# Moving the key eviction to the scalar engine and re-tuning the list scheduler's model in a hybrid attention, convolution and FFN block

## The chip, the cores and the metric

The kernel runs on all eight cores of one Trainium2 chip, two dies of four cores (0 to 3 and 4 to 7). Every core runs the same program on its own share: one of two batches, and eight blocks of 128 query positions. The metric is device microseconds of the slowest core.

Runs come in two states. In the fast one nearly all cores have a mean granted TensorE clock of 0.993 to 0.999 of full speed. In the slow one, one or both dies have a lower clock and the run is longer (31 of the 102 runs whose clocks are on record: 2725 to 3145 us, with the slowest core at a mean clock of 0.814 to 0.979). I compare fast runs only, and in traces I read cores of a die that was not slowed. "Ratio" below means the mean time of one kernel's fast runs over the mean of the kernel before's fast runs of the same rounds, so it is not quite the ratio of the medians that I quote.

Engine names: PE is TensorE (matmuls), PEld its weight loads, ACT the scalar engine, DVE the vector engine, POOL and SP issue DMAs. PSUM is the memory into which PE writes, used by this program as eight banks; "exp" is the exponential of the softmax, done by ACT.

## The reference, cut to what matters

```python
u = rmsnorm(h, ln1_g)
z = u @ w_in                      # conv inputs | q latent | kv latent | k rope | gates
y_conv = (zb * causal_dwconv3(zc * zv, conv_w)) @ w_conv_out
q  = rmsnorm(q_lat) @ w_q_b       # 16 heads x 192
kv = rmsnorm(kv_lat) @ w_kv_b     # per head: 128 key columns (nope), 128 value columns
q, k = rope(rmsnorm(q)), rope(rmsnorm(concat(k_nope, k_rope)))
y_mla = causal_attention(q, k, v) @ w_mla_out      # S = 4096
h = h + (gate_a * y_conv + gate_b * y_mla) @ w_o
h = h + (silu(a_gate) * a_up) @ w_down             # a = dwconv3(rmsnorm(h) @ w_up) + b
```

## The kernel before: the parts that matter here

Three stages follow each other on PE. The *input stage* makes the latents of all 4096 keys. The *attention stage* makes the query latents, then for 16 heads the keys, values, queries, 32 key blocks of attention, and in between the conv branch. The *static part* (gates, output projections, FFN) is emitted in a fixed order.

In the first two stages a list scheduler written in Python decides, while the program is built, in which order each engine gets its work. Every engine gets its queue in that order, and PE's trace follows it: on core 5 of the kernel before, the 18530 matmuls have the widths of the emitted order, one by one. The scheduler keeps a model of time: a cost for each instruction and a latency for each hand-over between engines.

```python
TAIL = {PE: 0.0, ACT: 0.115, DVE: 0.085, ...}
HOP = {PE: 0.147, ACT: 0.1, DVE: 0.1, ...}          # us from one engine's end to the next one's start
HOP_PE = {PE: 0.0, ACT: 0.3, DVE: 0.34, ...}        # from a matmul to its reader

class Flow:
    def post(self, horizon, once=False):            # give out waiting ACT/DVE work up to a horizon
        ...
                t = max(S.free[e], S.ready(e, rd, wr)) if e in (ACT, DVE) else 0.0
                key = (t - (0.3 if prio < self.first else 0.0), prio)      # the bonus: exps go first
        ...
    def go(self, step=None):                        # choose PE's next unit
        while any(s.units for s in self.order):
            self.post(S.free[PE] + 0.6)             # the horizon
            ...
                key = (int(max(0.0, t - S.free[PE]) / 0.1), u.pos)         # least waiting, then position
```

The streams in the attention stage are `s` (query-key products and their exp, with the mask), `p` (probabilities times values), `b` (the first query block and the ends of a head), and the *filler*: keys `k`, values `v`, queries `q` of the next head, and the conv `c`.

A key unit, before the change:

```python
        def KU(ct):
            ...
            for k in range(4):
                mm(PS[p], w[:, k, 0:128], cT[:, k, c0:c0 + 512], k == 0, k == 3, ...)
            cp(Kn[hb][:, c0:c0 + 512], PS[p], [TP[p]], [TKn[hb][ct]])      # DVE copy, PSUM to bf16
            kn = Kn[hb][:, c0:c0 + 512]
            tt(sqk[:, ct % 2, :], kn, kn, ALU.mult, ...)                   # DVE square
```

Of the kernel before, what the change touches and what calls it, by code (L numbers as in the profile page):

```python
# [10 lines left out]
AF = mybir.ActivationFunctionType  # L11
ALU = mybir.AluOpType

PE, ACT, DVE, POOL, SP = "tensor", "scalar", "vector", "gpsimd", "sync"
# [2 lines left out]


TAIL = {PE: 0.0, ACT: 0.115, DVE: 0.085, POOL: 0.1, SP: 0.0}
HOP = {PE: 0.147, ACT: 0.1, DVE: 0.1, POOL: 0.15, SP: 0.1}  # L20
HOP_PE = {PE: 0.0, ACT: 0.3, DVE: 0.34, POOL: 0.35, SP: 0.3}


def lag(o, eng):
    return HOP[eng] if o.is_dma else HOP_PE[eng] if o.eng == PE else TAIL[o.eng] + HOP[eng]

# [215 lines left out]
class Flow:  # L242
# [21 lines left out]
    def post(self, horizon, once=False):  # L264

        S = self.S
        while True:
            best = None
            for prio, s in enumerate(self.order):
                if not s.pend:  # L270
                    continue
                e, _, rd, wr = s.pend[0][:4]
                t = max(S.free[e], S.ready(e, rd, wr)) if e in (ACT, DVE) else 0.0
                key = (t - (0.3 if prio < self.first else 0.0), prio)
                if best is None or key < best[0]:
                    best = (key, t, s)
            if best is None or (best[1] > horizon and not once):
                return
            once = False
            e, fn, rd, wr, ch, c, marks, banks = best[2].pend.pop(0)  # L280
            S.add(e, fn, rd, wr, ch, c)
            for name, v in marks:
                self.pos[name] = v
            for b in banks:
                self.owner[b] -= 1
# [20 lines left out]
    def go(self, step=None):  # L306
        S = self.S
        while any(s.units for s in self.order):
            self.post(S.free[PE] + 0.6)
            best = None  # L310
            for s in self.order:
                if not s.units:
                    continue
                u = s.units[0]
                if (u.pe and len(s.pend) > 5) or (u.strict and s.pend) or (u.ok and not u.ok()):
                    continue
                t = S.ready(PE, u.need() if callable(u.need) else u.need, u.room) if u.pe else 0.0
                b = None
                if u.bank:
                    b, tb = self.bank_choice(s)  # L320
                    if b is None:
                        continue
                    t = max(t, tb)
                key = (int(max(0.0, t - S.free[PE]) / 0.1), u.pos)
                if best is None or key < best[0]:
                    best = (key, s, b)
            if best is None:
                assert any(s.pend for s in self.order), "nothing can go on"
                self.post(0.0, True)
                continue  # L330
            self.run(best[1], best[2])
            if step:
                step()
        self.post(1e9)
# [84 lines left out]
def build_program():  # L419
# [21 lines left out]
    PS = [psum[:, 512 * i:512 * i + 512] for i in range(8)]  # L441
    TP = [T("ps%d" % i, excl=True) for i in range(8)]
    S = Sched(nc)
# [4 lines left out]
    def V(off, shape, dt):  # L448
        nb = int(np.prod(shape)) * esz(dt)
        assert off % 4 == 0 and off + nb <= ARENA, (off, nb)  # L450
        v = arena[:, off:off + nb].bitcast(dt)
        if len(shape) == 2:
            v = v.rearrange("p (a b) -> p a b", b=shape[1])
        return v
# [47 lines left out]
    def width(ap):  # L502
        n = 1
        for d in ap.shape[1:]:
            n *= d
        return n

    def mm(out, lhsT, rhs, start, stop, reads, writes):
        S.add(PE, lambda e: e.matmul(out, lhsT=lhsT, rhs=rhs, start=start, stop=stop), reads, writes,  # L509
              cost=max(width(rhs) / 2400.0, 0.055) + 0.003)  # L510

    ptr = lambda x: 0.0 if x is None or isinstance(x, (int, float)) else 1.0

    def act(out, in_, func, reads, writes, **kw):
        c = width(out) / 1200.0 + (0.055 if any(t.excl for t in reads) else 0.105) + 0.09 * ptr(kw.get("scale", 1.0))
        S.add(ACT, lambda e: e.activation(out=out, in_=in_, func=func, **kw), reads, writes, cost=c)  # L516

    def dcost(out, *ins):
        fast = all(x.dtype == BF16 for x in (out,) + ins)
        return width(out) / (1920.0 if fast else 960.0) + 0.065  # L520

    def stt(out, in0, scalar, in1, op0, op1, reads, writes):
        S.add(DVE, lambda e: e.scalar_tensor_tensor(out=out, in0=in0, scalar=scalar, in1=in1, op0=op0, op1=op1),  # L523
              reads, writes, cost=dcost(out, in0, in1) + 0.065 * ptr(scalar))

    def tt(out, in0, in1, op, reads, writes):
        S.add(DVE, lambda e: e.tensor_tensor(out=out, in0=in0, in1=in1, op=op), reads, writes,  # L527
              cost=dcost(out, in0, in1))

    def ts(out, in0, s1, s2, op0, op1, reads, writes):  # L530
        c = dcost(out, in0) + 0.065 * ptr(s1)
# [7 lines left out]
    def cp(out, in_, reads, writes):  # L539
        S.add(DVE, lambda e: e.tensor_copy(out=out, in_=in_), reads, writes, cost=dcost(out, in_))  # L540
# [5 lines left out]
    def rsq(out, ssq, n, reads, writes):  # L546

        act(out, ssq, AF.Ln, reads, writes, scale=1.0 / n, bias=EPS)
        act(out, out, AF.Exp, writes, writes, scale=-0.5)
# [93 lines left out]
    CSq = V(cqo, [NA], F32)  # L643
    TCSq = S.region(cqo, NA * 4, "CSq")
# [14 lines left out]
    for i in range(3):  # L659
        v, t = P1.tile([16, 128], F32, "xw%d" % i)  # L660
# [57 lines left out]
    def cast(i):  # L718
        v, Tx = xtile(OWN_G[i])
        for q in range(2):  # L720
            act(v[:, 0, 8 * q:8 * q + 8, :], xo_[i % 3][:, 8 * q:8 * q + 8, :], AF.Copy, [Txo[i % 3]],
                Tx[0][2 * q:2 * q + 2])
        F1.mark("cast", i)
# [307 lines left out]
    def bank(n=5):  # L1031
        b = bk[0] % n
        bk[0] += 1
        return b
# [50 lines left out]
    for n in range(18):  # L1085
        i, t = divmod(n, 3)
        st_l.units.append(Unit(lambda i=i, t=t: ql(i, t), 2.6, need=Tu, pos=-9.0, bank=True))
        if n > 0:
            i, t = divmod(n - 1, 3)
# [7 lines left out]
    Kn, TKn, Vh, TVh = [], [], [], []  # L1097
    for i in range(2):
        v, t = P4.slabs(8, [512], BF16, "Kn%d" % i)
# [4 lines left out]
    for i in range(2):  # L1104
        v, t = P4.tile([NA], BF16, "Qn%d" % i)
        Qn.append(v)
        TQn.append(t)
        v, t = P4.tile([NA], BF16, "Qr%d" % i)
# [15 lines left out]
    qt2, Tqt2 = P4.tile([348], F32, "qt2")  # L1124
    qr_, Tqr_ = P4.tile([348], F32, "qr")
    ast, Tast = P4.slabs(2, [NA], BF16, "ast")
    for i in range(2):
        v, t = P4.slabs(8, [512], BF16, "Vh%d" % i)
# [18 lines left out]
    def fbank():  # L1147
        return F.bank
# [65 lines left out]
    def prologue_units(h):  # L1214
        hb = h % 2
        st = {}

        def start():
            if not st:
                st["wq"], st["Twq"] = wget(("hq", h))  # L1220
                st["wkv"], st["Twkv"] = wget(("hkv", h))

        def KU(ct):
            start()
            w, Tw = st["wkv"], st["Twkv"]
            p = fbank()
            c0 = ct * 512
            for k in range(4):
                mm(PS[p], w[:, k, 0:128], cT[:, k, c0:c0 + 512], k == 0, k == 3, [Tw] + TcTc(k, c0, 512), [TP[p]])
            cp(Kn[hb][:, c0:c0 + 512], PS[p], [TP[p]], [TKn[hb][ct]])  # L1230
            kn = Kn[hb][:, c0:c0 + 512]
            tt(sqk[:, ct % 2, :], kn, kn, ALU.mult, [TKn[hb][ct]], [Tsqk[ct % 2]])

# [35 lines left out]
        def QR(t):  # L1269
            start()  # L1270
            w, Tw = st["wq"], st["Twq"]
            off, n = QT[t]
            p = fbank()
            for k in range(6):
                mm(PS[p][:, 0:n], w[:, k, 128:256], qn[:, k, off:off + n], k == 0, k == 5, [Tw, Tqn[k]], [TP[p]])
            act(sqr[0:64, 0:n], PS[p][0:64, 0:n], AF.Square, [TP[p]], [Tsqr])
            tt(qt1[0:64, 0:n], PS[p][0:64, 0:n], CSq[0:64, off:off + n], ALU.mult, [TP[p], TCSq], [Tqt1])
            tt(qt2[0:64, 0:n], PS[p][64:128, 0:n], CSq[64:128, off:off + n], ALU.mult, [TP[p], TCSq], [Tqt2])
            tt(qr_[0:64, 0:n], qt1[0:64, 0:n], qt2[0:64, 0:n], ALU.add, [Tqt1, Tqt2], [Tqr_])

        def QS(t):
# [34 lines left out]
        for t in range(3):  # L1316
            qq += [Unit(U("q", QN, t), 0.87, ok=okq, bank=True), Unit(U("q", QR, t), 0.87, bank=True),
                   Unit(U("q", QS, t), 0.3, need=[Tsqn, Tsqr], strict=True, bank=True)]
# [149 lines left out]
    c = 0.0  # L1468
# [45 lines left out]
    for si in range(32 * NH):  # L1514
        h, kb = divmod(si, 32)
        c = 3 * (912 - A_(kb // 4)) / 2400.0
# [38 lines left out]
    for c in range(16):  # L1555
        for key, dst, Td, bo in (("ga", sga, Tsga, 0), ("gb", sgb, Tsgb, 16)):
            w, Tw = wget((key, c))
            for t, (off, n) in enumerate(T3):
                p = bank(8)
# [36 lines left out]
    for c in range(16):  # L1596
        w, Tw = wget(("wo", c))
        for t, (off, n) in enumerate(T3):
            p = bank()
# [21 lines left out]
    v, t = Pool_(A6, ARENA).slabs(11, [OWN], BF16, "fT0")  # L1621
    fT.append(v)
    TfT.append(t)
    v, t = PF.slabs(11, [OWN], BF16, "fT1")
# [174 lines left out]
```

## Time and profile before

| | |
|---|---|
| time before | 2699.5 us, median of 3 (2696.9 to 2701.5) |
| PE busy over the span (page of the slowest core, on the slowed die) | 96% |
| attention stage on an undisturbed core | 1022 to 1028 us |
| static part on such a core | 1445 us |

The first view lists each core's span and granted clock, and the median of each die.

```profile
core 4: 2688.2 us, clock 0.996
core 5: 2690.4 us, clock 0.997
...
die 0 (median of its cores): 2718.8 us, clock 0.982
die 1 (median of its cores): 2692.2 us, clock 0.996
```

So cores 4 to 7 are the ones to read. I use core 5.

The next view gives the busy time of each engine in one stretch, here exactly the attention stage of core 5 (from the start of its first query-latent matmul to the first gate matmul). Columns are named in the first line.

```profile
core 5: us, PE busy (x) PEld busy (x) DVE busy (x) ACT busy (x) POOL busy (x), PEclk, DMA share, GB/s
208.20:1230.30 1022.10, 982.00 (x7939) 605.58 (x7940) 807.56 (x1951) 624.12 (x1138) 32.73 (x62) 1.00 0.19 38
```

Two groups in the same stretch, by shape: the key copies on DVE and the value copies on ACT, the same shape on each engine (busy us, then mean ns of one, then idle time before them).

```profile
L540 DVE CAST arena<-ps 128x512 bf16<-128x512 f32 x128 | 87.6, 684 | 58.5 <-PE ps L509 57.5
...
L516 ACT ACTIVATE arena<-ps 128x512 bf16<-128x512 f32 x128 | 76.3, 596 | 86.6 <-PE ps L509 85.4
```

The waits in the same stretch (who waited for whom: us in total, times, longest), PE's and its weight loads':

```profile
PEld ps L509 <- issue: 139.5, 357, 1.9
...
PE ps L509 <- ACT arena L516: 15.3, 47, 1.0
...
PE ps L509 <- DVE arena L527: 11.7, 26, 1.2
...
PE ps L509 <- DVE arena L540: 5.3, 11, 0.9
PE ps L509 <- DVE arena L523: 2.3, 3, 1.8
```

L516 is the helper of every ACT activation, L527 of DVE tensor-tensor work, L540 of DVE copies, L523 of DVE scalar-tensor-tensor work.

### The profile page before, as it was taken

The numbers are of one execution on the slowest core, as the hardware profiler recorded it, in microseconds if no ns is written. First come the engines' busy times: TensorE is split into PE (matmuls) and PEld (weight loads), VectorE is DVE, ScalarE is ACT, GpSimd is POOL, SyncE is SP. The second block draws the span as 40 slices with busy tenths as digits, with TensorE's granted clock in tenths as the row PEclk, the third lists the DMA queues.
The fourth block names the chain that finished last, engine by engine and source line by source line (L and its number), as shares of the span: only waits on it lengthen the run. The fifth ranks groups of instructions, "written<-read, shape, count | busy, mean of one in ns | idle before, by whom it ended". The sixth has DMA issues, their size and how long they took to land.

```text
span 2743.0 us, 51305 instructions; the slowest of 8 cores (2688.2 to 2743.0 us)
## 1 busy us (share of the span) xinstructions
PE 2642.4 (96%) x18530; PEld 1659.0 (60%) x18530; DVE 1611.1 (59%) x3214; ACT 923.1 (34%) x1588; POOL 191.4 (7%) x330
## 2 busy tenths in 40 slices
PE   4999999999999999999999999999999999999996
PEld 3886655555555665555666666666556646655652
DVE  3772588888878888785111212257637736754752
ACT  5772366666656666662111112310000000000000
POOL 1010000000000000000000000000111110111010
PEclk9888899999999999999999999999999999999998
DMA  9573120031102031134444448444454444445455
GB/s 211 130 123 66 26 42 15 15 51 27 34 15 42 15 48 25 29 95 78 77 74 76 74 74 206 70 70 77 67 86 72 69 79 83 72 69 83 78 87 136
DMA packets 65686, 196.70 MB, mean 72 GB/s; under 512 B 7328, under 2 KB 8608, under 8 KB 64416
## 3 DMA queue, kind: packets, MB, share of 16 engines
q0 software_dynamic: 46800, 145.91, 33.6%
q1 hardware_dynamic: 18640, 47.51, 5.4%
q8 instruction: 155, 2.54, 0.4%
q14 instruction: 91, 0.75, 0.1%
HBM read 323.44 MB, written 15.83 MB: 124 GB/s over the span
## 4 chain that ended last, share of the span: by engine, by line
PE 85%; DVE 5%; ACT 3%; DMA 3%; issue 3%; SPq 0%; DVEq 0%; ACTq 0%; POOLq 0%
PE ps L509 85%; ACT arena L516 3%; DVE arena L527 3%; DMA outT<-arena 2%; DMA arena<-wkvin 1%; DVE arena L540 1%; DVE arena L523 1%; SPq L543 0%; DMA arena<-wall 0%; DVEq L196 0%; ACTq L196 0%; DVE arena L533 0%; DVE arena L536 0%; SPq L196 0%; ACT L516 0%
## 5 line engine op out<-in xcount | busy, mean ns | idle before, releaser
L509 PE MATMUL ps<-arena 128*128 128x390 bf16 (+9 forms) x18530 | 2642.4, 304 | 85.3 <-ACT arena L516 36.5
L509 PEld LDWEIGHTS ps<-arena 128*128 128x128 bf16 x18530 | 1659.0, 99 | 1068.3 <-issue 206.5
L527 DVE TENSOR_TENSOR arena<-ps,arena 128x390 f32<-128x390 f32 (+6 forms) x744 | 374.3, 510 | 843.6 <-PE ps L509 735.0
L527 DVE TENSOR_TENSOR arena<-arena 128x130 bf16<-128x130 bf16 (+22 forms) x1522 | 667.7, 479 | 140.7 <-ACT arena L516 108.0
L516 ACT ACTIVATE arena<-ps,arena 128x910 bf16<-128x910 f32 (+10 forms) x672 | 439.1, 673 | 486.5 <-PE ps L509 436.3
L516 ACT ACTIVATE arena<-arena 128x390 bf16<-128x390 f32 (+13 forms) x412 | 267.8, 674 | 912.9 <-DVE arena L523 796.6
L523 DVE SCALAR_TENSOR_TENSOR arena<-arena 128x1024 f32<-128x1024 f32 (+9 forms) x499 | 372.0, 761 | 34.3 <-ACT arena L516 8.5
L543 POOL DMA_DIRECT2D arena<-wall x294 | 171.1, 583 | 2362.8 <-PE ps L509 2303.5
L516 ACT ACTIVATE arena<-ps 128x512 bf16<-128x512 f32 (+12 forms) x499 | 236.4, 495 | 296.1 <-PE ps L509 290.3
L540 DVE CAST arena<-ps 128x512 bf16<-128x512 f32 x128 | 87.7, 685 | 68.6 <-PE ps L509 67.5
L536 DVE TENSOR_SCALAR arena<-arena 128x1024 f32<-128x1024 f32 (+1 forms) x90 | 72.3, 803 | 0.1
L523 DVE SCALAR_TENSOR_TENSOR arena<-ps,arena 128x256 bf16<-128x256 f32 (+1 forms) x80 | 33.3, 467 | 21.1 <-PE ps L509 13.4
L540 DVE COPY arena<-ps 128x456 f32<-128x456 f32 (+2 forms) x64 | 27.2, 424 | 8.0 <-PE ps L509 7.5
L543 POOL DMA_DIRECT2D arena<-xg x30 | 16.0, 549 | 153.7 <-ACT arena L516 59.5
L533 DVE TENSOR_SCALAR arena<-arena 128x390 f32<-128x390 f32 (+2 forms) x29 | 16.2, 560 | 2.3 <-DMA arena<-cst 0.7
L516 ACT ACT_TABLE_LOAD x5 | 6.4, 1283 | 28.1 <-DVE arena L523 14.2
L527 DVE TENSOR_TENSOR arena<-arena,ps 128x390 bf16<-128x390 f32 (+1 forms) x24 | 12.3, 514 | 3.0 <-PE ps L509 1.8
L540 DVE CAST arena<-arena 128x1028 f32<-128x1028 int32 (+1 forms) x5 | 3.6, 714 | 4.7 <-DMA arena<-posg 4.3
L540 DVE COPY arena<-arena 128x6 f32<-128x6 f32 (+1 forms) x24 | 3.8, 160 | 1.2
L961 POOL MEMSET arena<- 128x4096 bf16 x1 | 3.6, 3560 | 0.0
L1145 DVE MEMSET arena<- 64x1040 bf16 x2 | 1.9, 925 | 0.4 <-issue 0.4
L767 DVE MEMSET arena<- 128x128 bf16 x1 | 0.2, 165 | 1.2 <-PEq L420 1.2
(7 smaller groups left out, 1.9 us busy)
## 6 DMA issues: line engine op xcount, KB each, us to landing
arena<-wall POOLq DMA_DIRECT2D x182, 512.0 KB, 6.3
arena<-wall POOLq DMA_DIRECT2D x64, 352.0 KB, 5.2
arena<-xg POOLq DMA_DIRECT2D x22, 512.0 KB, 11.1
arena<-xo SPq DMA_DIRECT2D x16, 520.0 KB, 25.2
arena<-xg SPq DMA_DIRECT2D x8, 1024.0 KB, 7.1
arena<-wall POOLq DMA_DIRECT2D x32, 256.0 KB, 4.4
outT<-arena SPq DMA_DIRECT2D x32, 256.0 KB, 3.3
arena<-wall POOLq DMA_DIRECT2D x16, 384.0 KB, 5.6
```

The lines of the kernel that those rows point to most:

```text
L509: S.add(PE, lambda e: e.matmul(out, lhsT=lhsT, rhs=rhs, start=start, stop=stop), reads, writes, cost=max(width(rhs) / 2400.0, 0.055) + 0.003)
L516: S.add(ACT, lambda e: e.activation(out=out, in_=in_, func=func, **kw), reads, writes, cost=c)
L523: S.add(DVE, lambda e: e.scalar_tensor_tensor(out=out, in0=in0, scalar=scalar, in1=in1, op0=op0, op1=op1), reads, writes, cost=dcost(out, ...
L527: S.add(DVE, lambda e: e.tensor_tensor(out=out, in0=in0, in1=in1, op=op), reads, writes, cost=dcost(out, in0, in1))
L533: S.add(DVE, lambda e: e.tensor_scalar(out=out, in0=in0, scalar1=s1, scalar2=None, op0=op0), reads, writes, cost=c)
L536: S.add(DVE, lambda e: e.tensor_scalar(out=out, in0=in0, scalar1=s1, scalar2=s2, op0=op0, op1=op1), reads, writes, cost=c)
L540: S.add(DVE, lambda e: e.tensor_copy(out=out, in_=in_), reads, writes, cost=dcost(out, in_))
L543: S.add(eng, lambda e: e.dma_start(out=out, in_=in_), reads=reads, writes=writes, chan=chan, cost=in_.shape[0] * width(in_) * esz(in_.dtyp ...
L767: S.add(DVE, lambda e: e.memset(ones, 1.0), writes=[Tones], cost=0.2)
L961: f_h.units.append(Unit(lambda: S.add(POOL, lambda e: e.memset(krope, 0.0), writes=Tkr, cost=3.5), 0.0, pos=-8.0, ok=lambda: not f_w.units ...
L1145: S.add(DVE, lambda e, i_=i_: e.memset(Qr[i_][64:128, :], 0.0), writes=[TQr[i_]])
```

## The change

Its intent is to relieve DVE, which is the busier of the two helpers in the attention stage, and to give the scheduler latencies meant to be truer and a longer view. (In the attention stage of core 5 before, the median from the end of an ACT instruction to the start of one that waits for it is 102 ns on DVE and 144 ns on PE; the model's values for these go from 100 to 103 and from 147 to 150. That they come closer is so for DVE, and not for PE.)

```diff
-HOP = {PE: 0.147, ACT: 0.1, DVE: 0.1, POOL: 0.15, SP: 0.1}
-HOP_PE = {PE: 0.0, ACT: 0.3, DVE: 0.34, POOL: 0.35, SP: 0.3}
+HOP = {PE: 0.150, ACT: 0.103, DVE: 0.103, POOL: 0.15, SP: 0.1}
+HOP_PE = {PE: 0.0, ACT: 0.318, DVE: 0.343, POOL: 0.35, SP: 0.3}
...
-                key = (t - (0.3 if prio < self.first else 0.0), prio)
+                key = (t - (0.15 if prio < self.first else 0.0), prio)
...
-            self.post(S.free[PE] + 0.6)
+            self.post(S.free[PE] + 1.0)
...  (model costs of ACT and DVE instructions: +0.004 us each; +0.09 us for one DVE product)
-            cp(Kn[hb][:, c0:c0 + 512], PS[p], [TP[p]], [TKn[hb][ct]])
+            act(Kn[hb][:, c0:c0 + 512], PS[p], AF.Copy, [TP[p]], [TKn[hb][ct]])
```

Only the last pair of lines changes what an engine does. All the others change the order.

More of the change, by code (lines that the diff above doesn't have):

```diff
@@ L514, in act @@
     def act(out, in_, func, reads, writes, **kw):
-        c = width(out) / 1200.0 + (0.055 if any(t.excl for t in reads) else 0.105) + 0.09 * ptr(kw.get("scale", 1.0))
+        c = width(out) / 1200.0 + (0.059 if any(t.excl for t in reads) else 0.109) + 0.09 * ptr(kw.get("scale", 1.0))
         S.add(ACT, lambda e: e.activation(out=out, in_=in_, func=func, **kw), reads, writes, cost=c)
@@ L519, in dcost @@
         fast = all(x.dtype == BF16 for x in (out,) + ins)
-        return width(out) / (1920.0 if fast else 960.0) + 0.065
+        return width(out) / (1920.0 if fast else 960.0) + 0.069
     def stt(out, in0, scalar, in1, op0, op1, reads, writes):
@@ L524, in stt, with tt @@
               reads, writes, cost=dcost(out, in0, in1) + 0.065 * ptr(scalar))
-    def tt(out, in0, in1, op, reads, writes):
+    def tt(out, in0, in1, op, reads, writes, held=0.0):
         S.add(DVE, lambda e: e.tensor_tensor(out=out, in0=in0, in1=in1, op=op), reads, writes,
-              cost=dcost(out, in0, in1))
+              cost=dcost(out, in0, in1) + held)
     def ts(out, in0, s1, s2, op0, op1, reads, writes):
@@ L1277, in QR @@
             tt(qt1[0:64, 0:n], PS[p][0:64, 0:n], CSq[0:64, off:off + n], ALU.mult, [TP[p], TCSq], [Tqt1])
-            tt(qt2[0:64, 0:n], PS[p][64:128, 0:n], CSq[64:128, off:off + n], ALU.mult, [TP[p], TCSq], [Tqt2])
+            tt(qt2[0:64, 0:n], PS[p][64:128, 0:n], CSq[64:128, off:off + n], ALU.mult, [TP[p], TCSq], [Tqt2], 0.09)
             tt(qr_[0:64, 0:n], qt1[0:64, 0:n], qt2[0:64, 0:n], ALU.add, [Tqt1, Tqt2], [Tqr_])
```

## The prediction

> **What bounds it now.** TensorE. The page's busy table gives PE 96% of the span. The profiled execution fell in the slow state (die 0 clock 0.982, die 1 0.996), so I read core 4, span 2688.2 us at clock 0.996. In the stretches view PE is practically always busy from 1240 to 2600 us (the statically ordered gate, output and FFN part). From 0 to 240 us it idles about 40 us, mostly the start-up (named waits: ACT 20.8, first input DMA 14.1). The attention stretch, 240 to 1240 us, has PE busy 959 of 1000 us, DVE 804, ACT 616. So at most 41 us can be won there, 1.5% of the time. The waits view names about 36 of them in 88 waits: for ACT 15.3 us (47), for DVE tensor-tensor 11.7 (26), for the DVE copy 5.3 (11), for DVE scalar-tensor-tensor 2.3 (3). They are short (at most 1.8 us); DVE, 80% busy and often 100% for 10 us at a time, frees a bank or masks a tile late.
>
> **What the change does.**
> 1. 128 key evictions (128x512, PSUM to bf16) leave DVE, where the trace has 685 ns each, 87.6 us in all, and go to ACT, where the same shape (the value eviction) takes 596 ns, 76 us in all. DVE falls from 804 to about 716 us, ACT rises from 616 to about 692: nearly equal. [...]
> 2. The square of the keys stays on DVE but now needs a hand-over from ACT; the key sums sit off the tightest chain.
> 3. Model constants: costs +4 ns, hand-overs +3 to +18 ns, the exp stream's bonus 0.30 to 0.15 us, the horizon 0.6 to 1.0 us. No work changes, only the order in which engines get it.
>
> **On the critical path.** PE's own work does not change. Of the 41 us idle I expect about 12 to go: most of the 5.3 us on the DVE copy, half of the 14 us on other DVE work, a little by better order, less 2 to 4 us of new waits for ACT, since key copies of 0.6 us now stand in front of exps. The input stage, reordered too, gives 0 to 2 us. The rest stays.
>
> **Prediction.** 2688 us, range 2673 to 2703. Faster by over 2% would need 54 us, more than the attention stretch idles: 2%. Slower by over 2%: 1%. Within 2%: 97%.
>
> **What would show it.** (a) The 128 DVE casts gone, 128 more ACT 128x512 copies near 0.6 us; DVE 72%, ACT 69% in the attention stretch. (b) PE idle there falls from 41 to about 29 us on a die-1 core; the wait of PE for the DVE copy nearly gone, for DVE tensor-tensor halved, for ACT about equal or a few us more. (c) The static part the same to 2 us.
>
> **What would make it wrong.** ACT copies delay exps more than I think (wait for ACT at 25 us or more); a reordering that uses up the conv filler early and leaves the last heads bare; [...] or idle time that comes from the order of units rather than from late engines, when the horizon matters and the gain may reach 25 us.

The sum came to about 12 us in the attention stage (most of 5.3, half of 14, a little by order, less 2 to 4) and 0 to 2 us in the input stage; the forecast took 11.5 us off, 2699.5 to 2688. For DVE "often 100% for 10 us at a time": of 990 windows of 10 us in the attention stretch of core 4, one begun each us, 15 are over 99.5% and 127 over 95%.

## More of the kernel before

Filler needs a PSUM bank. Banks 6 and 7 are always for it, banks 1 and 3 only while the head stands at key blocks 20 to 27 (and bank 4 for a part of that time, cut here):

```python
            if 20 <= F.at("qk") % 32 <= 27:
                allowed += [1, 3]
```

The weight loads stand idle for 139.5 us in 357 places, far more than the 35 us that PE's own rows show.

## The result and the profile after

| | fast runs | ratio to before (95%) |
|---|---|---|
| changed kernel, first set | 2673.6 us (one of four timed runs; a further run had 2670.6) | 0.9899 (0.9875 to 0.9923) |
| changed kernel, run again beside before | 2671.0, 2674.1, 2665.8 us | 0.9889 (0.987 to 0.9907) |

So the change gains about 27 us, 1.0 to 1.1%, clear of noise. The median for the first set is 3009 us, because three of its four timed runs fell in the slow state (2924 to 3135 us, one or both dies at a clock of 0.82 to 0.93). The runs don't show this as a property of the change: in the experiments below the kernel before had slow runs of the same length (2973, 3053, 3084, 3085, 3109 and 3133 us, among others), and in the set of e5 to e8 it was slow in four of seven runs while e5 was fast in all four.

The profiled execution was slow on die 1. Die 0 was undisturbed; I use core 2.

```profile
core 2: 2664.3 us, clock 0.997
...
die 0 (median of its cores): 2665.0 us, clock 0.997
die 1 (median of its cores): 2914.3 us, clock 0.892
```

The granted clock in 40 slices of the span, in tenths, first core 4 of the changed kernel and then core 2:

```profile
PEclk8788888888888888888788889999999999999999
```

```profile
PEclk9999999999999999999999999999999999999999
```

The slow die runs its first 60% at about 0.8, and then recovers. The raw clock records behind this row say 0.8125 for about 1700 us on core 4, and at no time on core 2.

The attention stage of core 2, in the same views as before:

```profile
core 2: us, PE busy (x) PEld busy (x) DVE busy (x) ACT busy (x) POOL busy (x), PEclk, DMA share, GB/s
210.10:1203.00 992.90, 969.15 (x7940) 607.81 (x7940) 731.17 (x1823) 687.71 (x1266) 32.85 (x62) 1.00 0.20 39
```

```profile
L516 ACT ACTIVATE arena<-ps 128x512 bf16<-128x512 f32 x256 | 152.6, 596 | 75.2 <-PE ps L509 73.5
```

```profile
PEld ps L509 <- issue: 99.3, 281, 1.3
...
PE ps L509 <- ACT arena L516: 9.6, 26, 0.9
PE ps L509 <- DVE arena L527: 7.7, 19, 1.1
...
PE ps L509 <- DVE arena L523: 2.6, 5, 1.1
...
PE ps L509 <- DVE arena L540: 0.4, 2, 0.2
```

The whole gain lies in this stage: 1022 to 1028 us before, 992.8 us after (cores 1, 2 and 3 agree within 0.2 us). The static part took 1445 us on core 5 before and 1448 us on core 2 after; in other runs it differs by up to 11 us between cores of one kernel, so that is no effect of the change.

The busy row of PE shrinks too, from 982.0 to 969.2 us, although PE executes the same 7938 matmuls. That is one half of the miss.

**How much PE really loses.** I take PE's pace from its own starts. In the attention stage of core 5 before, these are the medians from the start of a matmul to the next start, for each of the 14 widths:

| columns | 1 | 64 | 128 | 130 | 194 | 260 | 276 | 324 | 344 | 348 | 390 | 454 | 456 | 512 |
|---|---|---|---|---|---|---|---|---|---|---|---|---|---|---|
| median, ns | 25 | 28 | 56 | 57 | 83 | 111 | 117 | 137 | 146 | 147 | 165 | 191.5 | 192 | 216 |

No single distance is more than 2 ns below its median. The static part of that core, in which PE's row is idle for 3.0 us, has the same medians for its three widths (260, 390 and 512), and there they add up to 1440.1 us where the starts add up to 1444.3 us. Core 2 after has the same medians within 0.5 ns. Over the 7938 matmuls of the attention stage they add up to 939.8 us, which I call the floor: an estimate from this one trace. What a stage takes beyond this is time in which a matmul began late. I split it into the idle time that the PE row shows and the rest, which hides inside "busy". It can hide there because the bars of neighbouring matmuls overlap: on core 5 before, a matmul of 390 columns is shown as 328 ns long on average, while the median distance between starts is 165 ns, so a start can be late by much of the difference without a gap in the row.

| attention stage, us | length | floor | idle of the PE row | late, inside busy |
|---|---|---|---|---|
| before, core 5 | 1022.0 | 939.8 | 40.1 | 42.2 |
| after, core 2 | 992.9 | 939.8 | 23.8 | 29.4 |

Half of the loss was invisible in the row that I took my ceiling from. The weight loads' busy share went from 605.6 of 1022.1 us (59.2%) to 607.8 of 992.9 (61.2%), about as it must when the same loads fill a stage that is 2.9% shorter. It does not say how much is lost: at the floor it would stand near 64% (my estimate, 605.6 of 939.8 us). Their idle time named "issue" went from 139.5 to 99.3 us (but see e13 for the limit of that number).

### The profile page after: what moved, and what is told of

The parts are those of the page before. It is cut to its first block, busy times and chain, and to the rows that moved or that the text cites. A ratio compares the mean times of both kernels' runs of the same rounds, so it can differ in the third digit from the quotient of the medians.

```text
span 2922.4 us, 51158 instructions; the slowest of 8 cores (2662.7 to 2922.4 us)
## 1 busy us (share of the span) xinstructions
PE 2841.3 (97%) x18415; PEld 1726.9 (59%) x18530; DVE 1534.9 (53%) x3086; ACT 983.2 (34%) x1716; POOL 191.8 (7%) x330
## 4 chain that ended last, share of the span: by engine, by line
PE 89%; DVE 4%; issue 3%; ACT 2%; DMA 2%; SPq 0%; DVEq 0%; ACTq 0%; POOL 0%; POOLq 0%
PE ps L509 89%; DVE arena L527 2%; ACT arena L516 2%; DVE arena L523 2%; DMA arena<-wkvin 1%; DMA arena<-xg 0%; SPq L543 0%; DVE arena L540 0%; DVEq L196 0%; ACTq L196 0%; DVE arena L533 0%; POOL arena L543 0%; POOLq L196 0%; SPq L196 0%
## 5 line engine op out<-in xcount | busy, mean ns | idle before, releaser
L509 PE MATMUL ps<-arena 128*128 128x390 bf16 (+11 forms) x18415 | 2841.3, 319 | 77.7 <-ACT arena L516 31.8
L509 PEld LDWEIGHTS ps<-arena 128*128 128x128 bf16 x18530 | 1726.9, 102 | 1191.5 <-issue 368.0
L527 DVE TENSOR_TENSOR arena<-arena 128x130 bf16<-128x130 bf16 (+18 forms) x1522 | 669.7, 479 | 249.1 <-ACT arena L516 223.2
L516 ACT ACTIVATE arena<-arena 128x256 f32<-128x256 f32 (+13 forms) x412 | 267.5, 674 | 1114.7 <-DVE arena L523 966.9
L516 ACT ACTIVATE arena<-ps,arena 128x128 bf16<-128x128 f32 (+10 forms) x672 | 440.7, 672 | 499.1 <-PE ps L509 464.3
L516 ACT ACTIVATE arena<-ps 128x512 bf16<-128x512 f32 (+13 forms) x627 | 312.8, 515 | 204.8 <-PE ps L509 198.9
L540 DVE COPY arena<-ps 128x456 f32<-128x456 f32 (+2 forms) x64 | 27.2, 425 | 2.1 <-PE ps L509 1.1
L540 DVE CAST arena<-arena 128x1028 f32<-128x1028 int32 (+1 forms) x5 | 3.6, 719 | 4.7 <-DMA arena<-posg 4.3
L540 DVE COPY arena<-arena 128x6 f32<-128x6 f32 (+1 forms) x24 | 3.8, 158 | 1.0
```

Of the source, the lines that this page charges most:

```text
L509: S.add(PE, lambda e: e.matmul(out, lhsT=lhsT, rhs=rhs, start=start, stop=stop), reads, writes, cost=max(width(rhs) / 2400.0, 0.055) + 0.003)
L516: S.add(ACT, lambda e: e.activation(out=out, in_=in_, func=func, **kw), reads, writes, cost=c)
L527: S.add(DVE, lambda e: e.tensor_tensor(out=out, in0=in0, in1=in1, op=op), reads, writes, cost=dcost(out, in0, in1) + held)
L540: S.add(DVE, lambda e: e.tensor_copy(out=out, in_=in_), reads, writes, cost=dcost(out, in_))
```

## The experiments

Theory A: the relief of DVE is the gain, so that banks and masks come sooner (my prediction's mechanism). Theory B: the new order is the gain. Theory C: each is worth little without the other. Each run's verdict rests on the length of the attention stage on undisturbed cores whose matmuls are all in the trace; one number stands for their median where they agree within 3 us, and otherwise the range is given.

All numbers, with the length that the scheduler itself planned for the stage (its own model, not a measurement):

| run | key copy on | order | planned | measured stage | ratio of totals (95%) |
|---|---|---|---|---|---|
| before | DVE | old | 1026 | 1022 to 1028 | 1 |
| e3 | ACT | old, unchanged | as before | 1024 to 1028 | 1.000 (0.9976 to 1.0024) |
| e8 | DVE, cut to 8 columns | old, unchanged | as before | 1015 to 1020 | (wrong values) |
| e1 | ACT | old constants, replanned | 1023 | 1019 | 0.9986 (0.9966 to 1.0005) |
| e2 | DVE | new constants | 1017 | 1006 | 0.9935 (0.9918 to 0.9952) |
| e4 | DVE | changed kernel's, unchanged | as changed | 1026 | 1.0004 (0.9985 to 1.0024) |
| e5 | ACT | horizon 0.6 | 1019 | 1005 | 0.9939 (0.992 to 0.9959) |
| e6 | ACT | bonus 0.28 | 1011 | 1003 | 0.9913 (0.9884 to 0.9941) |
| e7 | ACT | old latencies and costs | 1010 | 1004 | 0.9931 (0.9909 to 0.9954) |
| e9 | ACT | horizon 0.89 | 1011 | 999 | 0.9912 (0.9895 to 0.9928) |
| e10 | DVE | best of 400 settings | 1008 | 994 to 998 | 0.9909 (0.9893 to 0.9926) |
| e13 | ACT | filler held back | 1023 | 1013 | 0.9953 (0.9933 to 0.9973) |
| changed, e14 | ACT | new | 1004 | 993 | 0.9899, 0.9889 |
| e11 | ACT | searched setting a | 1001 | 992 | 0.9892 (0.9877 to 0.9906) |
| e12, e15 | ACT | searched setting b | 1002 | 989, 987 | 0.9871, 0.9876 |

Some settings made orders that the pre-run check, a simulation, refused with the message that PSUM would be read in the middle of an accumulation group. They were never run; I took neighbouring settings.

### e1: the key copy on ACT alone, planned anew with the old constants

```diff
-            cp(Kn[hb][:, c0:c0 + 512], PS[p], [TP[p]], [TKn[hb][ct]])
+            act(Kn[hb][:, c0:c0 + 512], PS[p], AF.Copy, [TP[p]], [TKn[hb][ct]])
-            self.post(S.free[PE] + 0.6)
+            self.post(S.free[PE] + 0.61)
```

> The kernel before with the key eviction on ACT and the planner's old constants (horizon 0.61 in place of 0.60, since at 0.60 the check refused the order that the planner made). Measure: the attention stage, from the first matmul of the query latents to the first of the gates, on a core of an undisturbed die (before 1022 to 1028 us, after 993). Theory A, the relief of DVE is the gain: 1000 to 1008 us, total about -20 us. Theory B, the new plan is the gain: 1020 to 1028, total within 5 us of before. Theory C, the two need each other: 1015 to 1022, total -5 to -10 us.

Measured: 1019 us, total 2695.0 us against 2699.3 us (means of fast runs). The stage is theory C's number, and not A's. The total, 4 us under before, is theory B's (within 5 us), and its interval includes 1. The horizon of 0.61 makes this one order among many (see e9), so I build nothing on e1 alone.

### e2: the new constants alone, key copy on DVE

```diff
 (the changed kernel)
-            act(Kn[hb][:, c0:c0 + 512], PS[p], AF.Copy, [TP[p]], [TKn[hb][ct]])
+            cp(Kn[hb][:, c0:c0 + 512], PS[p], [TP[p]], [TKn[hb][ct]])
```

> The changed kernel with the key eviction back on DVE, and the planner knows it: new constants, bonus and horizon alone. Theory A: attention stage 1020 to 1030 us, total as before. Theory B: 993 to 1005 us, total -20 to -28 us. Theory C: 1012 to 1020 us, total -5 to -12 us.

Measured: 1006 us, total 2681.3 us, 18 us under before. That lies 1 us outside theory B's band (993 to 1005) and well below C's (1012 to 1020): the new constants without any move have about 60% of the gain, with an order that is planned anew and is not the changed kernel's.

### e3 and e4: the engine changes, the order does not

To part the two causes for good, the scheduler plans as if the copy ran on one engine, and the instruction goes into the other's queue at the same place:

```diff
+def on(eng, f):
+    f.real = eng; return f
-        o = Op(eng, fn, is_dma, chan)
-        deps = {}
+        o = Op(getattr(fn, "real", eng), fn, is_dma, chan)
+        deps, o.plan = {}, eng            # plan: the engine of the time model
-        self.ops[eng].append(o)
+        self.ops[o.eng].append(o)
...  (e3, on the kernel before)
-            cp(Kn[hb][:, c0:c0 + 512], PS[p], [TP[p]], [TKn[hb][ct]])
+            S.add(DVE, on(ACT, lambda e, ...: e.activation(..., func=AF.Copy)), [TP[p]], [TKn[hb][ct]], cost=...)
...  (e4, on the changed kernel: planned for ACT, executed on DVE)
```

PE's order is then the same as in the kernel before (e3) or the changed one (e4); a comparison of the two programs showed no difference on PE.

> The order of the kernel before on every engine, unchanged, only the 128 key evictions stand in ACT's queue (at the place where the planner emitted them) and not in DVE's. PE's order is the same instruction by instruction. Theory A: most of the gain without any new plan, attention stage 1000 to 1010 us. Theory B: no gain, 1020 to 1035. Theory C: some, 1012 to 1022, since ACT's copies delay exps that the plan did not count on.

> The order of the changed kernel, but the 128 key evictions stand in DVE's queue. Theory A: the gain goes, 1022 us or more. Theory B: most of the gain stays, 995 to 1005 us. Theory C: worse than before, 1025 to 1045 us, because the order was planned for a DVE with 88 us less to do.

Measured for e3: 1026 us in the median of the cores (1024 to 1028), ratio 1.000 from two fast runs. The stretch and the waits of the attention stage in e3, core 0 (L1230 is the moved copy):

```profile
202.60:1228.70 1026.10, 983.65 (x7941) 606.66 (x7940) 736.45 (x1824) 689.94 (x1266) 32.86 (x62) 1.00 0.19 38
```

```profile
PEld ps L509 <- issue: 143.0, 361, 1.9
...
PE ps L509 <- ACT arena L516: 15.6, 46, 0.9
PE ps L509 <- DVE arena L527: 11.4, 24, 1.2
PE ps L509 <- ACT arena L1230: 4.5, 6, 1.0
...
PE ps L509 <- DVE arena L540: 3.2, 7, 1.3
PE ps L509 <- DVE arena L523: 2.9, 3, 1.8
```

DVE lost 71 us of busy time and ACT got 66, as intended, and PE waits as long as before. Its waits for the key copy only changed their name: 5.3 us for copies on L540 before, now 4.5 us for L1230 and 3.2 us for the copies that remain. The waits for other DVE work, which I had expected to halve, went from 11.7 to 11.4 us. The relief of DVE by the move, without a new order, gains nothing that can be seen: theory A falls.

Measured for e4: 1026 us on all six cores whose matmuls are all in the trace, ratio 1.0004. The stretch and PE's waits on core 0 (L1230 is the moved copy):

```profile
204.20:1230.30 1026.10, 977.62 (x7941) 607.16 (x7940) 804.98 (x1951) 620.35 (x1138) 32.86 (x62) 1.00 0.19 38
```

```profile
PE ps L509 <- DVE arena L527: 19.3, 48, 1.1
PE ps L509 <- DVE arena L523: 9.1, 16, 1.2
PE ps L509 <- ACT arena L516: 8.3, 25, 0.8
PE ps L509 <- DVE arena L1230: 7.2, 19, 1.5
```

PE now waits for DVE: 19.3 us for tensor-tensor work against 7.7 in the changed kernel, and 7.2 us for the key copy. The new order loses all its gain when DVE has to do the copies after all. It is theory C's lower edge, and at the same time A's "the gain goes". With e2 it says: an order is good for the load that it was planned for.

### e8: DVE relieved, and nothing given to ACT

```diff
-            cp(Kn[hb][:, c0:c0 + 512], PS[p], [TP[p]], [TKn[hb][ct]])
+            S.add(DVE, lambda e, ...: e.tensor_copy(out=<first n columns>, in_=<first n columns>), ..., cost=<of 512>)
+                                                     # n = 512 for heads 0 and 1, then 8: wrong on purpose
```

> The kernel before, same order on every engine, with the DVE key copies of all heads but the first two cut from 512 columns to 8 (wrong values on purpose; both buffers were filled by the first two heads). About 112 copies x 0.5 us = 56 us leave DVE and nothing is added to ACT. If DVE's lateness is what PE waits for and only ACT's new load hid it in the run with the old order: attention stage 1005 to 1015 us. If the order of the work sets the waits: 1018 to 1028 us, as before.

Measured: 1015 to 1020 us against 1022 to 1028, with DVE at 755 us of work on core 0. It lies mostly between my two bands. So 53 us less work on DVE in the old order gives some 8 us. That is a generous figure for relief: each of the 112 short copies takes about 0.47 us less (my estimate, the 53 us over 112), so it also hands its bank and its keys on earlier. In e3 the 8 us are not there. That ACT's added work takes them back is what the two runs suggest; no run shows it by itself.

### e5, e6, e7, e9: one part of the new constants put back, or nudged

```diff
e5:  -            self.post(S.free[PE] + 1.0)
     +            self.post(S.free[PE] + 0.6)
e6:  -                key = (t - (0.15 if prio < self.first else 0.0), prio)
     +                key = (t - (0.28 if prio < self.first else 0.0), prio)
e7:  old HOP, HOP_PE and instruction costs, horizon 0.99
e9:  -            self.post(S.free[PE] + 1.0)
     +            self.post(S.free[PE] + 0.89)
```

> The changed kernel with the horizon put back to 0.6 us. The planner itself now expects 1019 us for the attention stage (1004 with 1.0). If the chip follows the plan: 1005 to 1012 us, total -12 to -18 us against before. If the horizon alone carries the gain: 1018 or more, total within 8 us of before. If it does nothing: 993.

> The changed kernel with the exp stream's bonus at 0.28 us, near the old 0.30 (0.30 itself makes an order that the check refuses). The planner expects 1011 us. If the chip follows the plan: 998 to 1004 us, total -17 to -23 us. If the bonus carries the gain: 1015 or more.

> The changed kernel with the old hand-over latencies and instruction costs, bonus 0.15 us, horizon 0.99 us (1.0 makes an order that the check refuses). The planner expects 1010 us[...]. If the traced latencies make the plan truer: 1002 to 1010 us, total -10 to -18 us. If they do nothing: 993 to 996 us.

> The changed kernel with the horizon at 0.89 in place of 1.00 us, a step that is meant to matter little. The planner expects 1011 us (1004 with 1.00). If the gain is partly the luck of one order among many: attention stage 998 to 1004 us, 5 to 11 us longer than the changed kernel's. If it is the horizon's size: 993 to 996 us.

Measured: 1005, 1003, 1004 and 999 us. The first three follow the plan's band or miss it by less than 1 us, and e9 falls into the band that I had called luck. Putting any one part back costs 10 to 12 us, so none carries the gain alone. But the nudge of e9, which has no purpose, costs 6 us. The scheduler is chaotic at this scale: a small change of a constant makes another order, and orders differ by several us. Part of what each constant "gives" is therefore the luck of one order among many. Over 400 random settings of the scheduler, its planned stage had a median of 1016 us with the copy on ACT and 1027 with it on DVE, and a best of 1001 and 1008; the changed kernel's 1003.6 is close to the best. (These are plans made off the chip.)

### e10: the best order found for the copy on DVE

> Key eviction on DVE, planned with the new latencies and the best of 400 settings of the planner (bonus 0, bucket 0.05 us, queue limit 7, values' span 0.9): the planner expects 1008 us. If the move to ACT is needed for the whole gain: 996 to 1001 us, total -20 to -26 us against before. If a good order is all: 993 us or less, total as the changed kernel's.

Measured: 994 to 998 us, ratio 0.9909. A well chosen order alone has most of the gain. The move is still worth something: the best orders with the copy on ACT have 990 to 992 us (e11) and 987 to 989 us (e12, e15).

### e13: what the new order does differently

I counted the order that each kernel emits, by the key block at which the head's query-key products stand. A *bare* step is one with no filler between it and the query-key product before it (the short units of stream `b` are counted as filler here). The filler column is in the nominal PE time that the scheduler gives to each unit, stream `b` included. "Lost" is start-to-start time beyond the floor, from the trace (before on core 5, after on core 2, e13 on core 1, e15 on core 1):

| key blocks of a head | steps in all | bare: before, after, e13, e15 | filler on PE, us: before, after, e13 | lost, us: before, after, e13, e15 |
|---|---|---|---|---|
| 0 to 3 | 64 | 20, 17, 15, 16 | 47, 61, 65 | 13.8, 11.8, 13.5, 13.1 |
| 4 to 19 | 256 | 172, 67, 236, 86 | 124, 270, 6 | 34.0, 23.2, 42.1, 22.9 |
| 20 to 23 | 64 | 11, 10, 13, 15 | 219, 95, 361 | 11.1, 7.8, 9.3, 4.4 |
| 24 to 31 | 128 | 56, 39, 37, 33 | 88, 80, 75 | 21.4, 8.9, 7.2, 4.7 |

Before, filler was lumped into blocks 20 to 23, where extra banks are lent, and two of three steps in blocks 4 to 19 were bare. One head shows it. These are the stretches of head 6 for blocks 4 to 19 and then 20 to 23, first of the kernel before (core 5), then of the changed one (core 2):

```profile
641.00:658.50 17.50, 17.28 (x107) 8.61 (x106) 16.60 (x37) 14.51 (x21) 0.53 (x1) 1.00 0.22 46
658.50:686.00 27.50, 27.27 (x278) 19.02 (x277) 21.68 (x52) 14.82 (x31) 1.58 (x3) 1.00 0.19 40
```

```profile
635.00:671.50 36.50, 35.45 (x291) 21.79 (x290) 27.83 (x63) 24.28 (x40) 1.59 (x3) 1.00 0.18 32
671.50:678.10 6.60, 6.38 (x69) 4.24 (x68) 6.17 (x17) 5.22 (x12) 0.01 (x1) 1.00 0.45 94
```

Before, PE runs 107 matmuls in 17.5 us and then 278 in 27.5 us. In the first stretch DVE is busy 16.6 of 17.5 us and the weight loads only 49% of the time: PE goes from exp to exp with nothing between, and late hand-overs are a loss, though PE's row reads 99% busy. Of the 17.6 us from start to start 1.6 lie beyond the floor, where the row shows 0.2 us idle. After, the filler lies between the steps, and DVE has air (76%). (Here 1.9 of 36.4 us lie beyond the floor: one head shows the lumping, and only the sums over the heads show the gain.) In the kernel before some heads (4, 7, 8, 10, 11, 13) were already spread like that; in the changed one all are but heads 5 (in part) and 15.

To test it I made the changed kernel lump again, with everything else left alone:

```diff
     def bank_choice(stream):
         allowed = [6, 7]
+        if stream is not st_b and F.at("qk") >= 0 and 1 <= F.at("qk") % 32 // 4 <= 4:
+            return None, 0.0                     # no bank for filler at key blocks 4 to 19
```

> The changed kernel, but the projections and the conv get no bank while the query-key products stand at blocks 4 to 19 of a head, so that work (270 us in all in the changed kernel's order) moves mostly to blocks 20 to 23. If the spread of filler is how the new order gains: attention stage 1010 to 1025 us, total within 12 us of before. If the spread is a side effect: 993 to 1000 us, total as the changed kernel.

Measured: 1013.3 us, total 2689.1 us. The stretch and the weight-load wait of core 1:

```profile
207.10:1220.40 1013.30, 985.53 (x7940) 603.88 (x7940) 722.99 (x1823) 697.55 (x1266) 32.73 (x62) 1.00 0.20 38
```

```profile
PEld ps L509 <- issue: 146.6, 384, 1.3
```

Lumping costs 20.4 us of the 29 that the change had gained, and 18.9 of them are lost in blocks 4 to 19 (23.2 to 42.1 us). There 169 more steps are bare, so a bare step costs 0.11 us; between before and after it is 10.8 us for 105 steps, 0.10 us. PE's idle row hardly moved (23.8 to 27.8 us): four fifths of the loss hide inside busy. The weight loads' idle time named "issue" is no measure of it either: it is 146.6 us here, in a stage of 1013 us, and was 139.5 us before, in one of 1022 us.

So, with the copies on ACT, the spread of filler is shown to be how blocks 4 to 19 gain 10.8 us. It is not enough by itself. The same count over the traces of the frozen orders separates order and load:

| lost, us | order | key copy | key blocks 4 to 19 | key blocks 24 to 31 |
|---|---|---|---|---|
| before | old | DVE | 34.0 | 21.4 |
| e3 | old | ACT | 36.9 | 21.5 |
| e8 | old | DVE, cut short | 33.4 | 23.2 |
| changed | new | ACT | 23.2 | 8.9 |
| e4 | new | DVE | 38.6 | 8.6 |

(Cores 5, 0, 0, 2 and 0.) In blocks 4 to 19, e4 has the same 67 bare steps as the changed kernel and loses 15.4 us more: spread filler pays there only while DVE keeps up, and 0.1 us for a bare step holds for the orders that it was taken from. The largest single gain, 12.5 us at the ends of heads (blocks 24 to 31), goes with the order whichever engine makes the key copies: 20 to 24 us in every old-order trace that I counted, 8.5 to 8.9 us in every new-order one. Which feature of the order gives it stays open. There are fewer bare steps there (56 to 39, and 44 bare steps with 16.6 us in e2), but no experiment changed the head ends alone: that is a count, not a test.

### e11, e12, e14, e15: a better setting

The scheduler's own planned length ranks the orders fairly well (see the table), so I searched 1900 settings for a shorter plan. Setting b:

```diff
-                key = (t - (0.15 if prio < self.first else 0.0), prio)
+                key = (t - (0 if prio < self.first else 0.0), prio)
-                if (u.pe and len(s.pend) > 5) or ...
+                if (u.pe and len(s.pend) > 4) or ...
-                key = (int(max(0.0, t - S.free[PE]) / 0.1), u.pos)
+                key = (int(max(0.0, t - S.free[PE]) / 0.05), u.pos)
-        for us, span in ((kq, 0.85), (vq, 0.95), (qq, 0.85)):
+        for us, span in ((kq, 0.75), (vq, 0.95), (qq, 0.8)):
...  (PV's position offset 0.01 to 0.02)
```

> Key eviction on ACT and one of the best of 1900 settings of the planner (horizon 0.9, bonus 0.05, bucket 0.05, queue limit 6, spans 0.80, 0.85, 0.75): planned stage 1001.4 us against 1003.6. If the chip follows the plan: 989 to 992 us, total 1 to 4 us under the changed kernel's. If plans this close can't be told apart: 987 to 999 us.

> As the run before, another setting (horizon 1.0, bonus 0, bucket 0.05, queue limit 4, spans 0.75, 0.95, 0.80, PV offset 0.02): planned stage 1001.7 us. Same expectation: 989 to 992 us if the chip follows the plan, 987 to 999 us if plans this close can't be told apart.

> The changed kernel once more, for a fair comparison with the searched setting on the same chip: attention stage 993 us, total 2670 to 2674 us.

> The searched setting of e12 once more beside the changed kernel: attention stage 989 us, total 4 to 8 us under the changed kernel's if the difference is real, within 2 us of it if not.

Measured: setting a 992 us, setting b 989 us, and run again 987 us beside the changed kernel's 993. In totals the fast runs of b have 2664.1 to 2665.9 and 2665.3 to 2668.5 us. The changed kernel on the same chip as the last pair has 2665.8 to 2674.1 us. The stage is 4 to 5 us shorter in both traces. The totals' ratios, 0.9876 (two fast runs) and 0.9889 (three), have overlapping intervals, so the advantage in total time is not settled. (The ratios of e9 to e12 flatter all four a little: one of the eight fast runs of before in that set, 2726 us, is longer than the others, 2697 to 2703; it adds 0.1%.)

## Why the prediction was right or wrong

The class was right (within 2%). The size was wrong: I forecast 11.5 us (2699.5 to 2688), and the change gained 27. The fast runs (2665.8 to 2674.1) lie around the lower edge of my range (2673) or below it, and the median of 3009 us lies far above it for the reason of the slow state.

- **"So at most 41 us can be won there."** This step failed. It took PE's idle row for the whole loss. The stage lost 82.3 us beyond the floor, and 42.2 of them were late starts inside "busy". The change took 16.3 us from the idle row and 12.8 from the hidden part. The gain of 29 us stayed under the 41 all the same, so the ceiling alone doesn't explain the small forecast; the terms under it do (below).
- **"PE's own work does not change. Of the 41 us idle I expect about 12 to go."** The visible part was nearly right: 40.1 to 23.8. The busy row shrank by 12.9 us as well, which I had excluded.
- **"Most of the 5.3 us on the DVE copy, half of the 14 us on other DVE work, a little by better order."** This sum failed too: the attribution was upside down. In e3 the move without a new order gives nothing. A new order without the move gives 16 to 22 us of the stage (e2). Together they give 29 to 35. The "little by better order" was the term that was mis-sized: I gave it a few us at most, and the new constants alone measured 18 us of the total.
- **"Less 2 to 4 us of new waits for ACT."** The wait of PE for ACT fell, 15.3 to 9.6 us. It fell with the order and not with the move: it is 15.6 us in e3 (old order, copies on ACT) and 8.3 us in e4 (new order, copies on DVE).
- **What would show it.** (a) was right: the 128 casts are gone, ACT has 256 copies of 596 ns, DVE is at 73.6% and ACT at 69.3% of the stage (72% and 69% forecast). (b) The wait for the DVE copy is nearly gone (0.4 us), but the one for tensor-tensor work fell by a third and not by half. (c) The static part moved by 4 us, within the spread between cores.
- **What would make it wrong.** I named the right possibility last: idle time that comes from the order of units, with a gain of up to 25 us. (Of the others, none came: the wait for ACT fell, and the last head had 12 bare steps in blocks 4 to 19 against 16 before.) I gave it too little weight because I costed the one line of the diff that moves work, and treated the lines that move order as small since their numbers are small.

## What to carry to other kernels

Take the headroom of a PE-bound stage from start-to-start times against a floor, and not from the idle row of the matmuls: here half of the loss sat inside "busy". The idle time of the weight loads hints at it, but did not rank the orders here. When independent work is available to cover hand-overs, look at where in the loop it lies before moving work between engines; a step of attention with nothing beside it cost 0.1 us more here as long as the helpers kept up, and a new order was worth more than relieving the busier helper in the old one. An order made by a list scheduler fits the load it was planned for and jumps with small changes of its constants, so compare several orders before crediting a constant, and freeze the order when you want to know what an engine move does.
